# A weight's high and low parts for two blocks at once, where there is room for pairs of blocks

## The chip, the cores and the metric

The kernel runs on one core of one Trainium2 chip. The metric is the device time of one execution in microseconds, as the median of the runs.

## The reference

A backbone of two layers on 512 latent tokens and 256 context tokens, 1024 channels, all in float32. Layer 0 mixes the tokens with a bidirectional mLSTM, layer 1 with a bidirectional Mamba-2 SSD. Each layer ends with PEER, a channel mixer that picks for every token 16 of 16384 experts for each of 8 heads. Cut to the products in question:

```python
for i in range(DEPTH):                                   # 2
    ml, mc = modulation(c, ...), modulation(c_ctx, ...)  # silu(cond) @ ada_w[i] + ada_b[i], six rows each
    in_l, in_c = h_lat * (1 + ml[1]) + ml[0], h_ctx * (1 + mc[1]) + mc[0]
    # i = 0, mlstm: xm, z, o = h @ w_up; q, k = silu(conv(xm)) @ w_qk; v = xm @ w_v; ...; (...) @ w_down
    # i = 1, mamba2: z, xbc, dt = h @ w_in; ...; (...) @ w_out
    h_lat = layer_norm(ALPHA * h_lat + ml[2] * y_l, ...)
    h_lat = layer_norm(ALPHA * h_lat + ml[5] * peer_ffn(h_lat * (1 + ml[4]) + ml[3], ...), ...)
    # the context likewise, in layer 0 only

def block(xb):                                           # PEER, 128 tokens
    q = (xb @ wq).reshape(P_BLOCK, P_HEADS, 2, P_DK // 2)
    s = einsum('thcd,hcnd->thcn', q, sub_keys)           # 16 best keys of each half, then 16 best pairs
    act = gelu(einsum('td,thkd->thk', xb, u[idx]))
    return einsum('thk,thkd->td', gate * act, v[idx])
```

## The kernel before

**Products in three passes.** A float32 product is the sum of three passes of parts: an operand's high part is its value cast to fp32r, its low part is what is left. `mm3` (L211 to L213) issues high by high, high by low, low by high. So every weight is split on its way in. `wpair` (L169) does that for two blocks of 128 x 512 that one transfer brings: `raw2` (L152) allots one of three raw tiles [128, 2, 512] in the pool `wp` and starts the transfer on SP's queue (L155); then for each block by itself ACT casts the high part (`whi`, L176), and DVE or POOL subtracts it from the raw block (`wlo`, L178). A raw tile is free when its second subtraction is done.

**Room for parts.** `whi` and `wlo` are of one block each. There are three of each in `wp`, unless `more_parts` (L160) has opened a pool with more: `wpc` (9 blocks, L1441) for the context's first product, the modulation beside it and the context's w_v; `wpd` (9 blocks, L1428) for the latents' first product, which runs among the context's attention, so that the context's w_down and the context's wq use it too. The latents' last products take their first 16 blocks into the pool `dp` (`halves`, nb=16). The dense part of PEER takes v's blocks into three buffers of the pool `xp`.

**Which engine subtracts.** `los["eng"]` is a cycle of engines that each call of `next` moves on by one: "vvp" (two on DVE, one on POOL) in the context's first product and the modulation beside it (LO_U), DVE otherwise. uT's blocks of steps below 36 (UPX) go to POOL in both layers, and so do all of s_in's blocks of the context in layer 1 (SCP).

**Order.** Stages by the trace, in us: context's first product with modulation 45 to 268, its w_v to 372, its w_qk to 592; the context's attention with the latents' first product among it, then w_down and wq, to 1038; the latents' v, qk, attention and w_down to 2228, wq to 2424; PEER's prefix of layer 0 to 2905; its dense part to 3748; layer 1's context from 3735 to 3960, latents to 4515, wq to 4665; prefix to 5170, dense part to 6006. In a prefix (`peer_lat`, NPRE = 66 steps i2) the scores `u x` of 128 experts a step are made (`scores`, `mm3` with 128x384 outputs) while DVE picks the best pairs of every head (`select`, L829) and builds gate tables of one-hot products (L1012 to L1022, of which L1015 is POOL's); the fourth tile of tokens takes its experts' rows by gathers on POOL's queue (L860), weighted and added on DVE. In the dense part PE multiplies gated scores with v for all 128 steps, and makes the remaining 62 steps' scores. The planner that builds the program (`TileContext`) puts each engine's instructions in an order by its own estimate, with waits where a tile is reused. A pool opened with reuse_waits="tile" waits for single tiles of what lay on its bytes before; one without (those of `more_parts`) waits for every user of the pools that lay there.

## Time and profile before

| | us |
|---|---|
| median of three runs | 6019.12 |
| the three runs | 6018.73, 6019.12, 6024.26 |
| span of the profiled execution | 6006.3 |
| PE busy | 5316.2 (89%) |
| DVE busy | 4835.9 (81%) |
| ACT busy | 2269.3 (38%) |
| POOL busy | 2221.4 (37%) |
| cast to the high part (L176), 2032 instructions | 1227.3 |
| subtraction on DVE (L178), 1787 | 1245.3 |
| subtraction on POOL (L178), 245 | 340.6 |

The profile is of one execution on the chip; its span runs from the first to the last instruction. Busy times of different engines overlap, so they don't add up, and a share of the whole span is a mean over stages with different limits. What an instruction is worth is read in its stage: from what the other engines wait for there, and for how long.

### The profile page before, as it was taken

What the parts mean: (1) busy time and instruction counts of PE and PEld (TensorE: products, weight loads), DVE (VectorE), ACT (ScalarE), POOL (GpSimd) and SP (SyncE); (2) the same over time, 40 slices, a digit from 0 to 9 for tenths busy, and PEclk for the clock granted to TensorE, in tenths of its full rate; (3) what the DMA queues carried; (4) which work ended last, traced back from release to release, by engine and by line L of the source; (5) the groups of instructions that cost most, each with busy time, mean ns of one, the idle gap of its engine ahead of it and who ended that gap; (6) DMA issues with size and microseconds to landing.
All of it is one profiled execution on the core that took longest, in us unless ns stands there. A gap on an engine that the chain in (4) does not pass through costs nothing. (4 is left out here: it accounts for less than half of the span.)

```text
span 6006.3 us, 79377 instructions
## 1 busy us (share of the span) xinstructions
PE 5316.2 (89%) x25708; PEld 4369.6 (73%) x25708; DVE 4835.9 (81%) x11088; ACT 2269.3 (38%) x4219; POOL 2221.4 (37%) x1908
## 2 busy tenths in 40 slices
PE   6999999999997885888899999788878879799998
PEld 4788677766653464777778998676656779688997
DVE  6744668776677799999988988778877999798988
ACT  5543554232222332333333333443433334343333
POOL 1300001355534345564333445424341454433442
PEclk8999999999998897989999999799978989899999
DMA  6754455898879986456798999333334347898996
GB/s 215 248 183 163 155 181 158 296 332 299 310 249 322 339 304 224 138 168 201 256 343 315 349 335 328 100 95 104 99 103 127 105 142 228 275 345 318 342 342 234
DMA packets 655817, 1407.12 MB, mean 234 GB/s; under 512 B 62760, under 2 KB 237496, under 8 KB 650920
## 3 DMA queue, kind: packets, MB, share of 16 engines
q1 hardware_dynamic: 507944, 865.11, 42.9%
q0 software_dynamic: 147456, 536.94, 25.5%
q8 instruction: 202, 3.31, 0.2%
q14 instruction: 215, 1.76, 0.1%
HBM read 1278.10 MB, written 123.70 MB: 233 GB/s over the span
## 5 line engine op out<-in xcount | busy, mean ns | idle before, releaser
L176 ACT CAST whi<-raw 128x512 fp32r<-128x512 f32 x2032 | 1227.3, 619 | 1843.8 <-PE mm L212 614.4
L178 DVE TENSOR_TENSOR wlo<-raw,whi 128x512 fp32r<-128x512 f32 x1787 | 1245.3, 712 | 446.0 <-ACT whi L176 427.0
L860 POOL DMA_INDIRECT g<-in_u_dram,idx x512 | 638.8, 1248 | 1074.1 <-PE mx L213 276.8
L860 POOL DMA_INDIRECT g<-in_v_dram,idv x512 | 667.4, 1304 | 691.7 <-DVE acc L878 281.9
L878 DVE SCALAR_TENSOR_TENSOR acc<-g,act,acc 128x1024 f32<-128x1024 f32 x508 | 656.3, 1292 | 137.9 <-DMA g<-in_v_dram,idv 135.2
L867 DVE CUSTOM_DVE_ANT_0 g<-g,xb 128x1024 f32<-128x1024 f32 x512 | 626.3, 1227 | 149.4 <-DMA g<-in_u_dram,idx 148.4
L213 PE MATMUL sm<-pinh,wlo 128*128 128x384 f32 x2048 | 712.0, 349 | 30.3 <-POOL wlo L178 18.6
L211 PE MATMUL sm<-pinh,whi 128*128 128x384 f32 x2048 | 709.8, 347 | 5.8 <-ACT whi L176 3.6
L212 PE MATMUL sm<-pinl,whi 128*128 128x384 f32 x2048 | 705.5, 345 | 0.0
L178 POOL TENSOR_TENSOR wlo<-raw,whi 128x512 fp32r<-128x512 f32 x245 | 340.6, 1398 | 447.8 <-ACT whi L176 431.8
L829 DVE SCALAR_TENSOR_TENSOR oh<-iotc,bjf,g 128x50 f32<-128x50 f32 x1280 | 446.0, 397 | 0.2
L213 PEld LDWEIGHTS sm<-pinh,wlo 128*128 128x128 f32 x2048 | 395.6, 193 | 40.7 <-POOL wlo L178 22.5
L212 PE MATMUL mm<-wlo,wh 128*128 128x512 f32 x1024 | 399.6, 393 | 9.2 <-DVE wlo L178 9.2
L211 PEld LDWEIGHTS sm<-pinh,whi 128*128 128x128 f32 x2048 | 396.6, 194 | 12.8 <-ACT whi L176 4.7
L212 PEld LDWEIGHTS sm<-pinl,whi 128*128 128x128 f32 x2048 | 396.0, 193 | 5.5
L213 PE MATMUL mm<-whi,wl 128*128 128x512 f32 x1024 | 394.6, 392 | 3.1 <-DVE wl L189 3.0
L211 PE MATMUL mm<-whi,wh 128*128 128x512 f32 x1024 | 363.0, 396 | 33.6 <-ACT wh L188 29.5
L1015 POOL TENSOR_TENSOR oa<-oh,ct 128x512 bf16<-128x512 bf16 x192 | 249.5, 1310 | 293.7 <-DVE oh L1012 155.8
L212 PE MATMUL mm<-xcl,whi 128*128 128x256 f32 (+1 forms) x1024 | 349.0, 345 | 6.7 <-DVE xcl L189 6.7
L213 PE MATMUL mm<-xch,wlo 128*128 128x256 f32 (+1 forms) x1024 | 331.1, 348 | 21.7 <-DVE wlo L178 21.7
L211 PE MATMUL mm<-xch,whi 128*128 128x256 f32 (+1 forms) x1024 | 344.6, 349 | 5.0 <-ACT xch L188 4.0
L211 PE MATMUL mm<-inh,whi 128*128 128x512 f32 (+1 forms) x768 | 284.1, 374 | 9.7 <-ACT cva L404 4.9
(478 smaller groups left out, 11508.2 us busy)
## 6 DMA issues: line engine op xcount, KB each, us to landing
raw<-in_uT_dram SPq DMA_DIRECT2D x256, 512.0 KB
raw<-in_v_dram SPq DMA_DIRECT2D x256, 512.0 KB
raw<-in_w_qk_dram SPq DMA_DIRECT2D x128, 512.0 KB
raw<-in_ada_w_dram SPq DMA_DIRECT2D x96, 512.0 KB
raw<-in_w_up_dram SPq DMA_DIRECT2D x96, 512.0 KB
gD<-sg SPq DMA_DIRECT2D x48, 1024.0 KB
gtb<-gD SPq DMA_DIRECT2D x32, 1536.0 KB
raw<-in_s_in_dram SPq DMA_DIRECT2D x72, 512.0 KB
```

The lines of the kernel that those rows point to most:

```text
L176: nc.scalar.copy(hi, raw[:, u])
L178: (eng or next(los["eng"])).tensor_tensor(lo, raw[:, u], hi.bitcast(F32), OP.subtract)
L211: nc.tensor.matmul(o, sh, mh, start=start, stop=False)
L212: nc.tensor.matmul(o, sh, ml, start=False, stop=False)
L213: last["pe"] = nc.tensor.matmul(o, sl, mh, start=False, stop=stop)
L829: nc.vector.scalar_tensor_tensor(oh[:, k % 2], iotc, bjf[:, hd, k:k + 1], ci[:, hd], OP.is_equal, OP.mult, accum_out=fi[:, hd, k:k + 1])
L860: d = nc.gpsimd.indirect_dma_start(out=g_, out_offset=None, in_=tab, in_offset=bass.IndirectOffsetOnAxis(ap=ix[:, k:k + 1], axis=0))
L867: nc.vector.tensor_tensor_reduce(out=g_, in0=g_, in1=xb, scale=1.0, scalar=0.0, op0=OP.mult, op1=OP.add, accum_out=act[:, k:k + 1])
L878: nc.vector.scalar_tensor_tensor(acc, g_, act[:, k:k + 1], acc, OP.mult, OP.add)
L1015: (nc.gpsimd if GOP else nc.vector).tensor_tensor(oa, oh[:, 0], ct[:, 2, None, n].to_broadcast([P, P, 4]), OP.mult)
```

## The change

Where the parts go to a pool other than `wp`, `wpair` now makes them for both blocks of a transfer at once: one cast and one subtraction of 128 x 1024, into a `whi` and a `wlo` of [128, 2, 512], of which the two blocks are views. In `wp` they are made block by block as before. Pools count pairs now: `wpc` and `wpd` hold 4 pairs (WB = 4) for 9 blocks, `halves` 8 pairs for 16 blocks. New pools of pairs are opened: `wpq` (4) for the context's w_qk, `pw` (2) for PEER of the latents (wq and uT, in both layers), `scw` (2) for the context's s_in. `more_parts` restores the pool that was open before it. v's blocks go to `wp`. The cycle of engines moves on once for a pair. The diff, without comments that it takes out:

```diff
-WB = 9
+WB = 4
     def more_parts(es, name, bufs, side=None):
+        old = los.get("pool"), los.get("bufs")
         los.update(pool=es.enter_context(tc.tile_pool(name=name, bufs=1, side=side)), bufs=bufs)
-        es.callback(lambda: los.pop("pool"))
+        es.callback(lambda: los.update(pool=old[0], bufs=old[1]))
     def wpair(src, pool=None, eng=None, nb=None):
         raw = raw2(src)
-        pool = pool or los.get("pool", wp)
-        nb = nb or (los["bufs"] if pool is los.get("pool") else 3)
-        for u in range(2):
-            hi = pool.tile([P, 512], F32R, tag="whi", name="whi", bufs=nb)
-            nc.scalar.copy(hi, raw[:, u])
-            lo = pool.tile([P, 512], F32R, tag="wlo", name="wlo", bufs=nb)
-            (eng or next(los["eng"])).tensor_tensor(lo, raw[:, u], hi.bitcast(F32), OP.subtract)
-            yield hi, lo
+        pool = pool or los.get("pool") or wp
+        if pool is wp:
+            both = [(wp, 3, raw[:, u]) for u in range(2)]
+        else:
+            both = [(pool, nb or los["bufs"], raw)]
+        for pl, n, x in both:
+            hi, lo = [pl.tile(list(x.shape), F32R, tag=g, name=g, bufs=n) for g in ("whi", "wlo")]
+            nc.scalar.copy(hi, x)
+            (eng or next(los["eng"])).tensor_tensor(lo, x, hi.bitcast(F32), OP.subtract)
+            if pl is wp:
+                yield hi, lo
+            else:
+                for u in range(2):
+                    yield hi[:, u], lo[:, u]
@@ halves
-                        ws += wpair(wt[1, k:k + 2].rearrange("k p c -> p k c"), pool=dp, nb=16)
+                        ws += wpair(wt[1, k:k + 2].rearrange("k p c -> p k c"), pool=dp, nb=8)
@@ peer_lat
-        with tc.tile_pool(name="pt", bufs=1, reuse_waits="tile") as xp:
+        with tc.tile_pool(name="pt", bufs=1, reuse_waits="tile") as xp, ExitStack() as es_:
+            more_parts(es_, "pw", 2)
@@ dense
-            v = wpair(vs.rearrange("p (h c) -> p h c", h=2), pool=xp)
+            v = wpair(vs.rearrange("p (h c) -> p h c", h=2), pool=wp)
@@ ssd_ctx
-            with tc.tile_pool(name="scv", bufs=1, reuse_waits="tile") as q:
+            with tc.tile_pool(name="scv", bufs=1, reuse_waits="tile") as q, ExitStack() as es_:
+                more_parts(es_, "scw", 2)
@@ the context's w_qk
-    for _ in ml_qk(1, CTX):
-        pass
+    with ExitStack() as es_:
+        more_parts(es_, "wpq", WB)
+        for _ in ml_qk(1, CTX):
+            pass
```

## Rows read from the trace of the kernel before

**Rows 1.** The page: span; busy us (share), instructions of each engine.
```profile
span 6006.3 us, 79377 instructions
PE 5316.2 (89%) x25708; PEld 4369.6 (73%) x25708; DVE 4835.9 (81%) x11088; ACT 2269.3 (38%) x4219; POOL 2221.4 (37%) x1908
```

**Rows 2.** By stage: window, length; PE, PEld, DVE, ACT, POOL us; PEclk, DMA, GB/s.
```profile
45.00:268.00 223.00, 184.26 (x1092) 147.09 (x1093) 164.64 (x272) 127.34 (x255) 78.66 (x52) 0.91 0.69 223
...
2424.00:2905.00 481.00, 401.67 (x2374) 378.75 (x2373) 463.51 (x1622) 180.83 (x320) 258.40 (x255) 0.91 0.57 176
...
3500.00:3600.00 100.00, 100.00 (x504) 91.15 (x503) 89.69 (x109) 38.99 (x72) 47.36 (x36) 1.00 0.92 327
...
4665.00:5170.00 505.00, 428.11 (x2517) 401.81 (x2515) 489.70 (x1895) 186.07 (x333) 260.61 (x259) 0.91 0.55 171
...
3735.00:3960.00 225.00, 177.67 (x959) 147.97 (x958) 166.70 (x292) 100.74 (x205) 108.75 (x101) 0.85 0.35 117
```

**Rows 3.** Durations by line: count, ns min/median/max, first and last start, forms.
```profile
L176 ACT CAST whi<-raw x2032: 601/620/657, 8.5 to 5976.9; 128x512 fp32r<-128x512 f32 x185
...
L188 ACT CAST yh<-yfc x32: 394/406/410, 808.0 to 895.9; 128x256 fp32r<-128x256 f32 x32
...
L178 DVE TENSOR_TENSOR wlo<-raw,whi x1787: 631/685/1880, 9.1 to 5977.5; 128x512 fp32r<-128x512 f32 x199
...
L178 POOL TENSOR_TENSOR wlo<-raw,whi x245: 1252/1294/5399, 52.1 to 4947.4; 128x512 fp32r<-128x512 f32 x123
...
L1310 DVE TENSOR_TENSOR bcs<-bcs,dt_acs x32: 1206/1226/2054, 4004.5 to 4477.6; 128x1024 f32<-128x1024 f32 x32
...
L1140 POOL TENSOR_TENSOR S<-S,dt_eal x64: 605/796/2182, 3891.3 to 4453.3; 128x256 f32<-128x256 f32 x64
```

**Rows 4.** In order of time, 120 to 127: start, us, engine, line, what.
```profile
120.05 0.28 PE L211 MATMUL mm<-inh,whi 128*128 128x256 f32 x1
120.08 0.37 SPq L155 DMA_DIRECT2D raw<-in_w_up_dram  x1
...
120.17 0.28 PE L212 MATMUL mm<-inl,whi 128*128 128x256 f32 x1
...
124.15 1.14 ACT L176 CAST whi<-raw 128x512 fp32r<-128x512 f32 x2 [1.02 <-DMA raw<-in_w_up_dram]
...
124.81 1.29 DVE L178 TENSOR_TENSOR wlo<-raw,whi 128x512 fp32r<-128x512 f32 x2 [1.48 <-ACT whi L176]
...
126.13 0.37 SPq L155 DMA_DIRECT2D raw<-in_ada_w_dram  x1
```

**Rows 5.** The same, 2555 to 2559, of DVE and of POOL.
```profile
2555.81 1.33 DVE L829 SCALAR_TENSOR_TENSOR oh<-iotc,bjf,g 128x50 f32<-128x50 f32 x1
...
2558.32 0.26 DVE L829 SCALAR_TENSOR_TENSOR oh<-iotc,bjf,g 128x50 f32<-128x50 f32 x1
...
2555.78 2.54 POOL L178 TENSOR_TENSOR wlo<-raw,whi 128x512 fp32r<-128x512 f32 x2
```

**Rows 6.** Groups by line, 2424 to 2905: count, busy us, mean ns, idle before.
```profile
L829 DVE SCALAR_TENSOR_TENSOR oh<-iotc,bjf,g 128x50 f32<-128x50 f32 x411 | 161.8, 442 | 0.1
...
L178 DVE TENSOR_TENSOR wlo<-raw,whi 128x512 fp32r<-128x512 f32 x62 | 52.1, 842 | 1.5 <-ACT whi L176 1.5
...
L1015 POOL TENSOR_TENSOR oa<-oh,ct 128x512 bf16<-128x512 bf16 x90 | 116.6, 1307 | 147.7 <-PE mx L1022 55.4 <-DVE oh L1012 47.2 <-DVE oh L829 14.1
```

**Rows 7.** Who waited for whom, 45 to 268: us in total, times, longest.
```profile
ACT whi L176 <- DMA raw<-in_w_up_dram: 33.5, 29, 2.9
...
ACT whi L176 <- DMA raw<-in_ada_w_dram: 20.3, 15, 2.4
...
ACT whi L176 <- PE mm L212: 9.3, 10, 2.0
```

**Rows 8.** Groups by line, 3735 to 3960.
```profile
L178 POOL TENSOR_TENSOR wlo<-raw,whi 128x512 fp32r<-128x512 f32 x48 | 68.9, 1448 | 84.4 <-ACT whi L176 83.3 <-DVE st L408 0.3
```

## The prediction

> **What bounds the kernel now.** I read the page's first part, then the busy time by stage, then the groups by line, and at last single instructions. The page [rows 1] has PE busy 89% of the 6006.3 us and DVE 81%, which says little, since the stages differ [rows 2]. Two kinds of stage matter. In the dense stretches (3500 to 3600 stands for both layers) PE is busy the whole 100 us: preparation of weights is hidden there and can only lose. In the two prefixes (2424 to 2905 and 4665 to 5170) PE is busy 402 of 481 and 428 of 505 us, but DVE 464 of 481 and 490 of 505: there DVE is late last, and a microsecond off DVE is a microsecond off the stage. The reader should see two more: the context's first product (45 to 268) where no engine is full (PE 184 of 223, DVE 165), and the context's part of layer 1 (3735 to 3960) with PE 178 of 225, where every low part is made on POOL.
>
> Preparing weights costs 2032 casts and 1787 + 245 subtractions [rows 3]. By the code 1016 transfers of two blocks feed them. The change pairs 576 transfers (w_up of both streams 96, modulation 32, the context's w_v 32, w_qk 64, w_down 16, all wq 48, uT 256, the context's s_in 24, half of s_out 8) and leaves 440 in single blocks, among them all 256 of v. Of the 576 low parts POOL makes 123 (every third of the first 80, 72 of the prefixes, 24 of s_in), DVE 453.
>
> **The prices.** One cast: 620 ns at 512 elements and 406 at 256 [rows 3], so by that slope 0.62 + 2 x 0.214 = 1.05 us at 1024 (estimate). Two single casts in a row take 1.14 [rows 4], so a pair saves 0.09. A subtraction on DVE: two singles in a row take 1.29 us [rows 4]; one instruction of 1024 elements, two inputs and four-byte types takes 1.226, the median of L1310 [rows 3]. A pair saves 0.06. Taken alone the single lasts 0.685 [rows 3], and then it would be 0.144: the other end. I take 0.06, because in a stage where DVE is 97% busy its instructions stand in a row and overlap. On POOL: 1294 ns at 512, 796 at 256 [rows 3], so 1.294 + 2 x 0.498 = 2.29 at 1024 (estimate); two singles in a row take 2.54 [rows 5], and a pair saves 0.25. Over the kernel that is 53 us of ACT, 29 of DVE and 31 of POOL less busy time, nearly all of it where it isn't last.
>
> [...]
>
> **The prefixes.** 60 pairs go to DVE there (30 steps in each layer): 60 x 0.064 = 4 us less; ends 0 and 60 x 0.144 = 9. The POOL steps act on DVE too. A 128x50 step of L829 takes 0.26 us, but 1.33 when it begins with the first of two POOL subtractions in a row, and it ends as that one ends [rows 5]: POOL's instruction of 1.27 us keeps DVE's two-input instruction out for 1.07. In the first prefix L829 averages 442 ns over 411 instructions, so it loses 411 x 0.182 = 75 us, and L178 on DVE another 62 x 0.157 = 10 us; with 90 of L1015 [rows 6] and 72 subtractions (36 steps by two) that is 85 / 162 = 0.52 us for one POOL instruction. Two singles in a row keep DVE out for 2.14 us, one pair 2.29 - (1.27 - 1.07) = 2.09. So where DVE is pressing all the time 72 pairs give back 72 x 0.05 = 4 us. Ends: all of POOL's saved time comes to DVE, 72 x 0.25 = 18 us gained; or a single loses only its 0.52, that is 0.55 less than the full block, and the pair loses 2.09 - 0.55 = 1.54 against 1.04, 72 x 0.50 = 36 us lost. I take the 4, nearest to the row of two in a row.
>
> [...]
>
> Sum of the prefixes: 4 + 4 = 8 us less. PE there waits for DVE and POOL more than for itself, so what is late next is again DVE.
>
> **The context's first product.** Three raw buffers hold the transfers. One issued at 120.08 is cast at 124.15, its two subtractions run from 124.81 to 126.10, and the next transfer into that buffer goes at 126.13 [rows 4]: 1.95 us of holding, and no slack. ACT waits there for w_up's transfers 29 times and for modulation's 15 times, 54 us in all, for PE's release only 10 times [rows 7]. So the ring of three is late last in 44 of 80 transfers. With a pair the subtraction starts only when the whole cast is done: 1.05 + 0.04 + 1.23 = 2.32 on DVE, and 1.05 + 0.04 + 2.29 = 3.38 on POOL. Before, a transfer with a POOL block held 1.95 (first block) or 1.14 + 0.04 + 1.29 = 2.47 (second), and one on DVE alone 1.95: on average 2.12. After, (2 x 2.32 + 3.38) / 3 = 2.67. That is 0.55 more for each round of three, 0.18 for each transfer: 44 x 0.18 = 8 us lost. Ends: 0, if the buffered 4 pairs (8 blocks where there were 9) cover it, and 80 x 0.18 = 15. Queued behind a POOL pair's low part here are PE's modulation products, and behind those in PE's order the next products of w_up.
>
> **The context's part of layer 1.** POOL gets 24 pairs for 48 singles of 1448 ns [rows 8], 24 x (2.90 - 2.29) = 15 us less, and convolution steps on DVE are kept out less. Against it: there were three single buffers, now two pairs. PE needs 24 products of 0.12 us [rows 4], 2.9 us for a pair, and a buffer's round is 1.05 + 0.04 + 2.29 + 2.9 = 6.3, over two buffers 3.14: 0.26 more than PE wants, 24 x 0.26 = 6 us. I take 0, ends -8 (half of the 15) and +6.
>
> **The rest.** The context's v and qk stages, the latents' up and the peer's wq: PE or long chains are last, and 4 pairs or 2 pairs for 9 or 3 blocks change the depth little; 0, ends -6 and +6. Dense: 0, because PE is full; if that cover failed, 124 steps of a pair that comes 0.36 later would cost up to 45 us, but raw and weights there stand ready several us ahead, PE being full. The new pools (wpq, pw, scw) lie on bytes that earlier pools have left, and their first cast has to wait for those pools' last users; the trace doesn't show such a wait. Bounds: 0, or one cast and one subtraction uncovered at each of four openings, 4 x 2.3 = 9; I take 2. v's parts move from the peer's pool into wp, with three buffers again: 0. SP's queue has the same transfers in the same order; POOL's queue holds its gathers and L1015 behind a longer instruction, which is in the lock's ends above. The planner orders all queues anew; I have no row for that and leave 10 us either way.
>
> Sum: -8 + 8 + 0 + 0 + 2 = +2 us on the profiled execution. Its span is 6006.3 us and its own time lies within the three runs shown, 6018.73 to 6024.26, some 13 us above the span; the sum is set on their median, 6019.12, so 6021.
>
> **The rivals.** *Fixed costs count in full* (chance 0.28): every instruction saved on DVE in the prefixes is worth 0.144 us and POOL's shorter total comes to DVE, 9 + 18 = 27 us, with the first product unharmed: 5992. For it: DVE's 97%. Against it: the rows of instructions in a row, which overlap. [...] *The pair's low part comes late* (chance 0.30, slower): the first product of a pair waits for the whole cast and the whole subtraction. Its place is the context's first product, where the ring of three is the bound; from 2.12 us of holding on each further 0.1 us costs 0.03 us a transfer, and if all 80 are bound so, 15 us; s_in's two buffers add 6; with no gain in the prefixes 6040. For it: 54 us of waits for transfers. Against it: in the other 36 transfers something else is late. *The change doesn't do what it says where it would count* is part of the forecast: v's 256 transfers, a quarter, stay single, and the paired uT of the dense stretches lies under a full PE.
>
> **How the numbers follow.** Within 0.2% (12 us, about what a measurement of this kernel can tell from no change) has 0.42 and is the forecast, 6021; faster 0.28, slower 0.30. The range reaches to both rivals and the planner's 10 us beyond part of them, 5994 to 6046; what is left out, the lock's 36 us and an uncovered dense stretch, I put at under 2 in 10. The forecast's own range is 6007 to 6031.
>
> **What would show it.** Right: casts of 128x1024 near 1.05 us, subtractions near 1.23 on DVE and 2.29 on POOL; DVE's busy time in the prefixes down by some 2 to 6 us each, with L829 at an unchanged mean; the stretch from 45 to the first w_v product some 8 us longer, with more waiting of ACT for transfers; dense stretches as long as before. Wrong: prefixes shorter by over 10 us each (then a pair blocks DVE less than its length says), or longer with L829 above 480 ns (then the longer lock costs), a first product that is no longer, or dense stretches in which PE waits for low parts.

## The result: slower by 1.0%

The changed kernel takes 6069.76 us (median of four runs, 6062.91 to 6072.6) against 6018.92 of the kernel before beside it: a ratio of 1.0099, 95% interval 1.0082 to 1.0116. (The ratio is the measurement's own; the quotient of the two medians is 1.0084, and one of the four runs of before took 5989.46 us where the other three took 6018.73 to 6024.26.) The forecast was 6021, with 5994 to 6046 as its range: the time lies outside, on the slower side. The page of after, its first lines:

```profile
span 6061.1 us, 77541 instructions
PE 5328.7 (88%) x25708; PEld 4361.0 (72%) x25708; DVE 4817.8 (79%) x10635; ACT 2186.3 (36%) x3643; POOL 2200.9 (36%) x1785
```

Beside [rows 1], ACT has lost 83 us of work, DVE 18, POOL 21 (forecast 53, 29 and 31), and the span is 55 us longer. Line numbers of after are 3 to 9 higher: the cast L176 is L180, the subtraction L178 is L181, the products L211 to L213 are L218 to L220, `select`'s L829 is L836, L1015 is L1023, L1022 is L1030 and the transposes of inputs L316 are L323; in the experiments they are higher by a few more. The instructions cost what was forecast, but for POOL's. Durations by line, as in [rows 3]:

```profile
L180 ACT CAST whi<-raw x1456: 602/622/1080, 8.7 to 6031.6; 128x512 fp32r<-128x512 f32 x109, 128x1024 fp32r<-128x1024 f32 x73
...
L181 DVE TENSOR_TENSOR wlo<-raw,whi x1334: 642/693/3355, 9.4 to 6032.3; 128x512 fp32r<-128x512 f32 x125, 128x1024 fp32r<-128x1024 f32 x66
...
L181 POOL TENSOR_TENSOR wlo<-raw,whi x122: 2330/2396/4427, 52.7 to 4991.7; 128x1024 fp32r<-128x1024 f32 x122
```

A pair on POOL takes 2.396 us (forecast 2.29), so it saves 0.14 us against two singles in a row ([rows 5], 2.54) and not 0.25. The 576 casts of pairs alone have a mean of 1.047 (forecast 1.05).

**Where the time went.** I cut both traces at the first product of each stage on PE, so that a stage lasts from its own first product to that of the next. The table has these lengths for the stages that matter, in us. "b2" is a second trace of the kernel before, from the experiments: what it differs by from the first is what a difference must exceed.

| stage | before | b2 | after |
|---|---|---|---|
| context's first product, modulation | 201.5 | 201.9 | 221.7 |
| context's w_v | 100.8 | 100.8 | 105.0 |
| context's w_qk, up to the second tile of the latents' input | 237.5 | 237.9 | 243.5 |
| context's attention, and its w_down | 258.9 | 258.8 | 262.2 |
| latents' w_qk | 590.4 | 584.9 | 590.5 |
| prefix, layer 0 | 500.8 | 498.9 | 507.3 |
| prefix, layer 1 | 489.1 | 489.5 | 492.2 |
| dense with v alone, both layers | 555.9 | 549.1 | 572.1 |
| dense with scores, both layers | 1066.4 | 1064.8 | 1058.9 |
| context of layer 1 | 233.6 | 231.8 | 236.8 |

So the largest loss of one stage is the context's first product, the prefixes are longer where they should be shorter, and a dozen microseconds are lost where pools open. Two traces of one program differ by 5 to 7 us in the latents' w_qk and in the dense stretch with v alone, so of those little can be said from one trace; the first product, w_v, w_qk and the prefixes repeat within 2 in these two. (Six kernels that are like after up to there scatter by 6 in the first product, as shown below, so one length of it is good to some 6.) The windows of after, columns as in [rows 2]:

```profile
70.00:292.00 222.00, 190.30 (x1104) 150.12 (x1103) 143.86 (x211) 117.21 (x174) 62.64 (x25) 0.96 0.64 207
...
2469.00:2976.00 507.00, 406.47 (x2418) 383.23 (x2416) 491.81 (x1773) 173.36 (x266) 255.34 (x221) 0.88 0.58 179
3560.00:3660.00 100.00, 100.00 (x504) 90.20 (x503) 86.45 (x93) 36.40 (x59) 45.83 (x35) 1.00 0.94 337
4732.00:5225.00 493.00, 403.20 (x2397) 377.17 (x2396) 472.97 (x1734) 166.90 (x259) 245.80 (x222) 0.91 0.58 177
```

and the same stretches of before, cut in the same way:

```profile
75.00:276.00 201.00, 183.38 (x1100) 148.50 (x1100) 150.97 (x261) 123.28 (x249) 75.42 (x50) 0.97 0.70 227
...
2440.00:2941.00 501.00, 402.39 (x2411) 379.99 (x2410) 482.70 (x1739) 185.83 (x330) 259.83 (x256) 0.89 0.59 180
4690.00:5179.00 489.00, 403.11 (x2395) 380.99 (x2393) 468.10 (x1763) 179.75 (x323) 258.04 (x257) 0.90 0.57 178
```

In the first product every engine that prepares weights has less to do than before, and the stretch is 21 us longer, with 207 GB/s for 227: nothing is full, something waits. In the dense stretch PE is busy all 100 us as in [rows 2]. In the prefixes DVE, the engine that should gain, is busy for 9 and 5 us more (in layer 0 with work of the stage ahead, see PEER).

### The profile page after: what moved, and what is told of

Read it like the earlier page. It is cut to its first block, busy times and chain, and to the rows that moved or that the text cites. A ratio compares the mean times of both kernels' runs of the same rounds, so it can differ in the third digit from the quotient of the medians.

```text
span 6061.1 us, 77541 instructions
## 1 busy us (share of the span) xinstructions
PE 5328.7 (88%) x25708; PEld 4361.0 (72%) x25708; DVE 4817.8 (79%) x10635; ACT 2186.3 (36%) x3643; POOL 2200.9 (36%) x1785
## 5 line engine op out<-in xcount | busy, mean ns | idle before, releaser
L180 ACT CAST whi<-raw 128x512 fp32r<-128x512 f32 (+1 forms) x1456 | 1137.5, 789 | 1584.9 <-PE mm L219 560.1
L181 DVE TENSOR_TENSOR wlo<-raw,whi 128x512 fp32r<-128x512 f32 (+1 forms) x1334 | 1176.2, 891 | 426.2 <-ACT whi L180 405.7
L885 DVE SCALAR_TENSOR_TENSOR acc<-g,act,acc 128x1024 f32<-128x1024 f32 x508 | 674.0, 1327 | 147.2 <-DMA g<-in_v_dram,idv 143.3
L220 PE MATMUL sm<-pinh,wlo 128*128 128x384 f32 x2048 | 707.4, 346 | 14.6 <-POOL wlo L181 10.1
L218 PE MATMUL sm<-pinh,whi 128*128 128x384 f32 x2048 | 705.2, 344 | 16.4 <-ACT w L985 15.0
L181 POOL TENSOR_TENSOR wlo<-raw,whi 128x1024 fp32r<-128x1024 f32 x122 | 303.3, 2488 | 460.2 <-ACT whi L180 424.7
L836 DVE SCALAR_TENSOR_TENSOR oh<-iotc,bjf,g 128x50 f32<-128x50 f32 x1280 | 444.6, 398 | 0.1
L218 PEld LDWEIGHTS sm<-pinh,whi 128*128 128x128 f32 x2048 | 397.9, 194 | 25.3 <-ACT w L985 17.3
L220 PEld LDWEIGHTS sm<-pinh,wlo 128*128 128x128 f32 x2048 | 398.0, 194 | 23.4 <-POOL wlo L181 13.4
L220 PE MATMUL mm<-whi,wl 128*128 128x512 f32 x1024 | 399.4, 396 | 0.0
L218 PE MATMUL mm<-whi,wh 128*128 128x512 f32 x1024 | 364.5, 398 | 26.1 <-ACT wh L195 20.4
L220 PE MATMUL mm<-xch,wlo 128*128 128x256 f32 (+1 forms) x1024 | 346.4, 348 | 24.2 <-DVE wlo L181 24.0
L1023 POOL TENSOR_TENSOR oa<-oh,ct 128x512 bf16<-128x512 bf16 x192 | 243.9, 1281 | 330.6 <-DVE oh L1020 214.4
L218 PE MATMUL mm<-xch,whi 128*128 128x256 f32 (+1 forms) x1024 | 349.3, 349 | 4.8 <-ACT xch L195 4.8
L1030 PE MATMUL mx<-og,oa 128*128 128x128 f16 x1536 | 206.9, 296 | 109.4 <-DVE og L1025 86.7
```

The costliest lines, as they stand in the source:

```text
L180: nc.scalar.copy(hi, x)
L181: (eng or next(los["eng"])).tensor_tensor(lo, x, hi.bitcast(F32), OP.subtract)
L218: nc.tensor.matmul(o, sh, mh, start=start, stop=False)
L220: last["pe"] = nc.tensor.matmul(o, sl, mh, start=False, stop=stop)
L836: nc.vector.scalar_tensor_tensor(oh[:, k % 2], iotc, bjf[:, hd, k:k + 1], ci[:, hd], OP.is_equal, OP.mult, accum_out=fi[:, hd, k:k + 1])
L885: nc.vector.scalar_tensor_tensor(acc, g_, act[:, k:k + 1], acc, OP.mult, OP.add)
```

## The experiments

Each kernel is timed beside the kernel before on its own chip, whose median went from 5999 to 6019 us between chips; so ratios are compared, not times. Where a variant keeps single blocks in a pool, `more_parts` gets a last argument `False` and `wpair` runs its old loop for that pool. I begin with the measure of a trace.

**b2.** The kernel before, unchanged.

> The kernel before, unchanged, for a second trace of it. What the stages of two traces of one program differ by is the size below which a difference between stages says nothing. If the trace shown was an ordinary one, every stage agrees within 3 us, and the stages that are longer in the changed kernel and its variants by 4 to 7 us (w_v, the context's w_down, both prefixes) stay so against this trace too. If it was a lucky one, those differences go.

1.0001 (0.9985 to 1.0017). The table above has its stages: w_v, w_down and the prefixes stand, two stages scatter by 5 to 7 us, more than the 3 expected.

### The context's first product

**u_c.** The changed kernel with nine single blocks in `wpc`.

```diff
-    more_parts(wpc, "wpc", WB, "right")
+    more_parts(wpc, "wpc", 9, "right", False)
```

> The changed kernel, with the context's first product, the modulation beside it and the context's w_v again in nine single blocks; all else as changed. Theory A (three raw buffers are the bound of that stretch, and a pair holds one longer): the stretch from the first to the last product with the context's input falls from 208 back to near 186 us, and the time by 20 to 24, to about 6048. Theory B (the loss of 50 us is spread over all stages, by the planner's new order): the time stays within 8 us of 6070.

1.0076 (1.0059 to 1.0092): a quarter of the loss. The stretch is 203.3 us by the cut of the table (the expectation's 208 and 186 are of another cut): the loss of this place is the pairs' and is gone with them. But three quarters of the whole stay, so it is spread over other places too, as theory B has it: neither alone holds. w_v stays at 104.6 although its blocks are single again, so that its 4 us are not the pairs' of w_v.

**ring4.** A fourth raw buffer in a pool of its own while `wpc` is open.

```diff
+        rp_ = next(ring) if "xpool" in ring_ else wp     # every fourth transfer: the pool "rw", one buffer
-        raw = wp.tile([P, 2, 512], F32, tag="raw", name="raw", bufs=3)
+        raw = rp_.tile([P, 2, 512], F32, tag="raw", name="raw", bufs=3 if rp_ is wp else 1)
```

> The changed kernel with a fourth raw buffer while the context's first product, modulation and w_v run, pairs kept. Theory A (the ring of raw buffers): with four in turn the waits of ACT for transfers fall, the stretch loses 15 to 25 us, about 6050. Rival (PE waits for the whole cast and the whole subtraction of a pair, however early the transfer is there): no gain in the stretch, 6065 to 6075, and PE's waits for low parts as before.

1.0075 (1.0058 to 1.0091), the stretch 199.8 us: with pairs as they are, one more raw buffer gives back all that they cost. The rival (PE waits for late parts whatever the transfers do: no gain) falls as the account of the whole; with four buffers pairs still take 9 us more than single blocks (b_r4, below). Waits of ACT for transfers from 45 us to near the end of this stretch (284 and 271), of after

```profile
ACT whi L180 <- DMA raw<-in_w_up_dram: 36.3, 27, 3.8
...
ACT whi L180 <- DMA raw<-in_ada_w_dram: 30.2, 26, 5.0
```

and of ring4 (us in total, times, longest):

```profile
ACT whi L185 <- DMA raw<-in_w_up_dram: 17.0, 14, 5.6
...
ACT whi L185 <- DMA raw<-in_ada_w_dram: 14.4, 12, 5.0
```

66.5 us of waiting in after ([rows 7]: 53.8 before) and 31.4 with four buffers.

**c_v.** The changed kernel with no low part on POOL there.

```diff
-LO_U = "vvp"
+LO_U = "v"
```

> The changed kernel with no low part on POOL in the context's first product and the modulation beside it (the cycle vvp made v). Theory A: a POOL pair holds its raw buffer 3.6 us, always the same one of three, a DVE pair 2.3 when POOL is quiet; with DVE alone the mean hold falls from 3.3 to 2.4 and a round of the three buffers from 8.5 to about 7.4, so the stretch loses 20 us: 6050. Rival (DVE becomes the bound when it makes all 80 low parts, 27 of them more, 33 us on top of some 165 busy in 222): no gain, 6065 to 6075.

1.0073 (1.0048 to 1.0098), the stretch 197.3 us. DVE has room for all low parts (busy 129.6 of the 180 us from 70 to 250), so the rival falls. Groups by line and form, DVE's pairs in the stretch (70 to 284 and 70 to 268), of after

```profile
L181 DVE TENSOR_TENSOR wlo<-raw,whi 128x1024 fp32r<-128x1024 f32 x50 | 70.3, 1413 | 59.2 <-ACT whi L180 54.1 <-PE mm L226 5.0
```

and of c_v:

```profile
L182 DVE TENSOR_TENSOR wlo<-raw,whi 128x1024 fp32r<-128x1024 f32 x78 | 95.1, 1220 | 50.0 <-ACT whi L181 46.4 <-PE mm L221 3.1
```

1.220 us without POOL (forecast 1.23), 1.413 with it: a pair on POOL holds DVE's pairs up as well as its own buffer. One round of after shows it, in order of time on each queue and engine:

```profile
176.99 0.38 SPq L155 DMA_DIRECT2D raw<-in_w_up_dram  x1
...
178.19 0.38 SPq L155 DMA_DIRECT2D raw<-in_ada_w_dram  x1
...
179.70 0.37 SPq L155 DMA_DIRECT2D raw<-in_w_up_dram  x1
...
181.51 1.05 ACT L180 CAST whi<-raw 128x1024 fp32r<-128x1024 f32 x1 [3.10 <-DMA raw<-in_w_up_dram]
182.86 1.05 ACT L180 CAST whi<-raw 128x1024 fp32r<-128x1024 f32 x1 [0.30 <-DMA raw<-in_ada_w_dram]
184.36 1.05 ACT L180 CAST whi<-raw 128x1024 fp32r<-128x1024 f32 x1 [0.46 <-DMA raw<-in_w_up_dram]
...
182.69 2.36 POOL L181 TENSOR_TENSOR wlo<-raw,whi 128x1024 fp32r<-128x1024 f32 x1 [5.72 <-ACT whi L180]
...
183.94 3.33 DVE L181 TENSOR_TENSOR wlo<-raw,whi 128x1024 fp32r<-128x1024 f32 x2 [4.27 <-ACT whi L180]
...
185.08 0.37 SPq L155 DMA_DIRECT2D raw<-in_ada_w_dram  x1
...
186.16 0.37 SPq L155 DMA_DIRECT2D raw<-in_w_up_dram  x1
187.30 0.37 SPq L155 DMA_DIRECT2D raw<-in_ada_w_dram  x1
```

Three transfers go out within 2.7 us, then none for 5.4, until POOL's pair ends at 185.05 and frees its buffer; DVE's two pairs take 3.33 us where two at 1.22 would take 2.44.

**res9.** Every third pair on POOL as before, but not always in the same buffer.

```diff
-LO_U = "vvp"
+LO_U = "vvpvpvpvv"
```

> The changed kernel with the same share of POOL in the context's first product, every third pair, but in the order vvpvpvpvv, so that POOL's pair falls into each of the three raw buffers in turn and not always into the same. Theory A1 (the ring goes at the pace of its slowest buffer, since SP's queue issues in order and every POOL pair comes to the same buffer): a round falls from 8.5 to near 7.7 us and the stretch loses 12 to 18 of its 20 us. Theory A2 (the mean hold of a pair sets the round, as in my sum): the mean hold is the same, the stretch within 4 us of 222.

1.0082 (1.0063 to 1.0101), the stretch 213.6 us. Six kernels whose program is that of after up to here (after, u_w, w_split, w_half, w_s4, u_s) have 215.4 to 221.7, mean 218.4: some 5 us won, which is neither theory's number. That POOL always meets the same buffer is a small part at most.

**b_v, b_r4, b_v_r4.** The kernel before, single blocks everywhere, without POOL there (the edit of c_v), with the fourth raw buffer there (the edit of ring4), and with both.

> The kernel before, single blocks everywhere, with no low part on POOL in the context's first product and the modulation beside it. If the ring of three raw buffers sets that stretch (a transfer with a POOL block holds its buffer 2.5 to 3.2 us, one on DVE alone 1.95 when it need not wait), the mean hold falls from 3.0 to 2.4, a round from 7.8 to 7.1, and the stretch loses 14 to 20 us against before: a ratio of 0.997. If DVE becomes the bound with 53 more subtractions (36 us), nothing is won or up to 10 us lost: 1.000 to 1.002.

> The kernel before with the fourth raw buffer in the context's first product, modulation and w_v, and POOL left in (vvp). If the ring is late there whoever subtracts, the stretch falls from 202 to some 186 us, as it did by taking POOL out, and the ratio to before is 0.997; if POOL's blocking of DVE is what counts and not the ring, it stays above 196, and 1.000.

> The kernel before with single blocks everywhere, no POOL in the context's first product and modulation, and a fourth raw buffer there. If the ring is still what is late there with DVE alone, the stretch falls from 186 (before 202) by another 5 to 10 us; if PE, which needs 173 us, and ACT's and DVE's chains are now late, by under 4. In the whole time a gain of 0.1 to 0.4% against before, if the planner's new order gives nothing back; the kernel without the fourth buffer showed 0.9995 although its stretch was 16 us shorter.

b_v: the stretch 185.8 us, 16 shorter than before as expected, yet 0.9995 (0.9982 to 1.0008) in the whole: other stages gave it back, and which did is not to be told from stages that scatter by 5 to 7. b_r4: 190.8 us, between its two expectations, and 0.9972 (0.9962 to 0.9982). b_v_r4: 181.7 us, 4 below b_v and so near the end of "under 4", and **0.9971** (0.9960 to 0.9982), with b_r4 the fastest of all, 0.3% below the kernel before and without a single pair.

The ring in numbers. For some 70 transfers of each kernel, from 66 us to 240 to 264 (before its stretch ends): how long a transfer holds its buffer (from its first cast to the end of its last subtraction), the time from its issue to its first cast, and the time from its issue to that of the third after it, all means in us.

| kernel | hold | issue to cast | three transfers | stretch |
|---|---|---|---|---|
| before | 3.04 | 4.59 | 7.76 | 201.5 |
| after | 3.28 | 5.05 | 8.51 | 221.7 |
| u_c, single blocks | 3.10 | 4.57 | 7.83 | 203.3 |
| c_v, pairs, no POOL | 2.49 | 4.89 | 7.41 | 197.3 |
| b_v, single, no POOL | 2.46 | 4.59 | 7.09 | 185.8 |
| b_v_r4, and four buffers | 2.79 | 5.89 | 6.57 | 181.7 |

80 transfers pass: (8.51 - 7.76) / 3 x 80 = 20 us, as measured; for b_v (7.09 - 7.76) / 3 x 80 = -18, measured -16. For c_v it gives -9, measured -4, and for b_v_r4 -32, measured -20: there the ring is no longer all that is late. u_w, whose program is that of after here, has 3.28, 4.72 and 8.17, so the time from issue to cast scatters too. Pairs and single blocks without POOL hold a buffer alike, and still c_v is 11.5 us longer than b_v: its casts come 0.3 us later after the issue. ACT's waits for PE to leave a buffer don't explain it, 11.8 us in c_v over this stretch against 9.3 in before [rows 7]; it stays open.

### Where pools open

**q_right.** `wpq` on the other side of the memory.

```diff
-        more_parts(es_, "wpq", WB)
+        more_parts(es_, "wpq", WB, "right")
```

> The changed kernel with the pairs' pool of the context's w_qk (wpq) on the other side of the memory, so that it doesn't lie on the bytes where the latents' input is loaded. Theory C (on the left side it keeps the latents' first loads until w_qk is over): the transposes of the latents' input no longer wait 22 us in all at the start of that stage but 10 to 14, and the time falls by 6 to 10 us, about 6062. If the pool's place doesn't matter: within 4 us of 6070.

The w_qk stage falls from 243.5 to 237.4, as expected, and with it the transposes' wait shown below; the time does not show it, 1.0114 (1.0097 to 1.0131) against 1.0099. The mechanism in order of time, in after:

```profile
623.71 0.64 SPq L1418 DMA_DIRECT2D res<-in_x_dram  x1
...
631.16 1.23 DVE L318 TENSOR_TENSOR big<-res,row 128x1024 f32<-128x1024 f32 x1 [0.41 <-DMA res<-in_x_dram]
...
633.70 1.97 PE L323 MATMUL sm<-ident,big 128*128 128x128 f32 x8 [11.69 <-DVE big L319]
```

and in before the same loads:

```profile
7.12 0.44 SPq L1409 DMA_DIRECT2D res<-in_x_dram  x1
66.85 0.33 SPq L1409 DMA_DIRECT2D res<-in_x_dram  x1
```

Before, the latents' first tiles were loaded 600 us ahead. With `wpq` on the left their place is taken until w_qk is over, and PE stands 11.69 us. All kernels with the first load near 7 us (before, b2, q_right, u_d, d5, b_v, b_r4, b_v_r4, best) have 233.7 to 238.0 us for w_qk, the ten with it after 600 us 241.3 to 248.5: 7 us, by the place of a pool. But the early loads have a price at the start, among the transfers that the first product waits for. With three raw buffers it begins at 73.4 to 77.1 us in the six kernels that load early (75.8 in q_right) and at 67.5 to 70.3 in the nine that load late (70.3 in after). So some 6 of the 7 us come back there, which fits that the time of q_right shows nothing.

The 4 us of w_v come from the same pool, but not from its place (q_right keeps them, 104.3). In order of time at its end, of after

```profile
388.54 2.94 ACT L180 CAST whi<-raw 128x1024 fp32r<-128x1024 f32 x3
...
391.38 1.07 ACT L529 COPY vT<-sm 128x512 f32<-128x512 f32 x2
392.51 3.59 PE L466 MATMUL sm<-vT,wgv 128*16 128x256 f32 x8 [1.80 <-ACT vT L529]
```

and of before:

```profile
373.50 0.59 ACT L522 COPY vT<-sm 128x512 f32<-128x512 f32 x1 [0.71 <-PE sm L1130]
...
374.46 0.59 ACT L522 COPY vT<-sm 128x512 f32<-128x512 f32 x1 [0.37 <-PE sm L1130]
374.94 1.02 ACT L188 CAST xch<-st 128x256 fp32r<-128x256 f32 x3
375.10 1.90 PE L459 MATMUL sm<-vT,wgv 128*16 128x256 f32 x8 [0.26 <-ACT vT L522]
```

Before, w_qk's first blocks went to `wp` and were made while w_v ran. Now the casts of three pairs stand in ACT's queue ahead of the copies that the gates need, and PE waits for those, 1.80 us for 0.26. The rest is a wait of 0.82 us for w_qk's first product, and PE's 453 products of w_v keep it busy for 102.4 us where they took 100.5, at a mean granted clock of 0.97 for 1.00. Kernels with `wpq` have 104.2 to 105.8 us for w_v, those without 100.8 to 103.3.

**u_d and d5.** The latents' first product, the context's w_down and its wq in nine single blocks, and in five pairs.

```diff
-                more_parts(es_, "wpd", WB)
+                more_parts(es_, "wpd", 9, None, False)         # u_d
+                more_parts(es_, "wpd", 5)                      # d5
```

> The changed kernel with the latents' first product, the context's w_down and its wq again in nine single blocks. If four pairs are too few where three streams of weights share them, the stretch of the context's w_down (110 us before, 116 or 117 with pairs) comes back to 110 or 111 and the ratio to before falls by 0.001, to 1.009. If that stretch is longer for another reason: 116, and 1.010.

> The changed kernel with five pairs in place of four for the latents' first product, the context's w_down and its wq. If the stretch of the context's w_down is 116 to 117 us and not 110 because four pairs are too few for two streams of weights, it falls to 111 to 113. If a pair's parts come too late there whatever the depth, 116.

u_d: 1.0074 (1.0046 to 1.0102); d5: 1.0089 (1.0072 to 1.0105). The w_down stretch comes back in both, 110.8 and 110.6 us for 116.8. But it was not the loss that I took it for. Windows of this stretch, of before, after and d5:

```profile
810.00:920.00 110.00, 103.03 (x449) 82.48 (x447) 75.16 (x146) 60.79 (x119) 2.15 (x1) 0.98 0.60 192
```

```profile
832.00:949.00 117.00, 111.18 (x473) 89.45 (x473) 74.82 (x125) 60.64 (x95) 1.94 (x1) 0.97 0.60 188
```

```profile
832.00:942.00 110.00, 103.91 (x453) 83.43 (x451) 70.96 (x118) 55.65 (x89) 1.35 (x1) 0.99 0.60 189
```

PE has 473 instructions in it in after, 449 and 453 in the others: work of the latents' product that ran in the stage ahead (the context's attention, 3 us shorter in after) came over. With that stage the difference is 3 us. Both kernels' larger pool also lets the latents' loads go at 7 us again, and their w_qk takes 233.7 and 236.7.

**mend.** Pairs in layer 0's first stages alone, no POOL and four raw buffers in the first product, `wpq` on the right, five pairs for the latents: the edits of c_v, ring4, q_right and d5 in one, without `pw` and `scw`, with sixteen single blocks in `halves` and v in `xp`.

> Pairs only in layer 0's first stages (context's first product, modulation, w_v, w_qk, latents' first product, context's w_down and wq), with each cause of loss found there taken away: no POOL and a fourth raw buffer in the first product, wpq on the other side, five pairs for the latents; PEER, s_in and s_out in single blocks as before. If ring, place and depth are the causes, the context's first product, w_v and w_qk together fall to 520 to 526 us (before 540, changed 570), the latents' loads are issued near 7 us again, and the ratio is 0.996 to 0.999. If the pair as such costs there, it stays over 1.000. Single blocks with the fourth buffer and no POOL had 523 us and 0.9971: pairs save nothing beyond that unless this goes below.

0.9975 (0.9963 to 0.9986). First product, w_v and w_qk together take 533.8 us: 6 less than before (539.8), 36 less than after (570.1), but 11 more than the single blocks of b_v_r4 with the same ring (523.1). The latents' loads went at 584 us only, so the place was not mended. With ring and POOL alike, pairs still cost 7 us in the first product (189.0 against 181.7); in the whole time mend and b_v_r4 are not told apart.

### PEER

**u_w, w_split, w_half, w_s4.** The changed kernel without the pool `pw` (v in `xp`, as before); with POOL's part of a pair in two subtractions; with every engine's part in two; and with four single blocks on the bytes of the two pairs.

```diff
-            more_parts(es_, "pw", 2)
+            more_parts(es_, "pw", 4, None, False)          # w_s4
     (in wpair, for the pool pw; in w_split where the engine is POOL, in w_half always)
-            e.tensor_tensor(lo, x, hi.bitcast(F32), OP.subtract)
+            for u in range(2):
+                e.tensor_tensor(lo[:, u], x[:, u], hi[:, u].bitcast(F32), OP.subtract)
```

> The changed kernel without the pool of pairs in PEER (pw): wq and uT in single blocks in wp, v in three buffers of xp, as before; all else as changed. If the pairs are what makes the prefixes longer (501 to 507 us and 489 to 493), both fall back, by 6 and 4 us, the two stretches with scores lose the 4 us each that they won, and the time stays within 6 us of the changed kernel's ratio to before, 1.010. If POOL's longer lock costs (the upper end of my range, 36 us), the ratio falls to 1.005 or less. If the prefixes are longer by the planner's order alone, they stay at 507 and 493.

> The changed kernel in which POOL's part of a pair in PEER (72 pairs of uT) is worked out as two subtractions of 512 elements; cast and DVE's pairs as changed. Theory P1 (the prefixes are longer since POOL's 2.4 us instruction holds back what is queued behind it, the gate tables' products L1023 on POOL above all): the prefixes come back from 507 and 493 to some 501 and 489. Theory P2 (the pair's parts come later and two pairs hold no more than four blocks, so PE and the tables collide whatever POOL's grain is): they stay at 505 to 508 and 492 to 495. The time itself moves too little to tell, 0 to 10 us.

> The changed kernel with every low part in PEER's pool of pairs worked out in two halves, on DVE as on POOL; only the cast is of 1024. If PE's waiting for a whole subtraction makes the prefixes longer, they come back to 501 and 489; if two pairs are too shallow, so that the cast of a pair waits until PE has done with all of the pair two before, they stay at 505 to 508 and 492 to 495.

> The changed kernel with its pool for PEER (pw) on the same bytes and v in wp, as changed, but with four single blocks in it where two pairs were, each cast and subtracted by itself. Theory W1 (the pair as such: its parts come late and whole, in a pool of two): the prefixes come back, 507 to some 501 and 493 to some 489, and the stretches with scores lose their 3 us. Theory W2 (the pool's place, or v in wp): the prefixes stay at 505 to 508 and 492 to 495. Ratio to before 1.006 under W1 as in the kernel without the pool, 1.010 under W2.

| | ratio | prefix, layer 0 | layer 1 |
|---|---|---|---|
| 8 kernels without `pw` in the prefix | | 500.0 (498.5 to 502.7) | 489.5 (489.1 to 490.2) |
| 11 kernels with pairs in `pw` | | 507.5 (502.8 to 512.5) | 493.6 (492.1 to 495.6) |
| u_w | 1.0061 (1.0036 to 1.0085) | 499.5 | 489.4 |
| w_split | 1.0102 (1.0084 to 1.0120) | 509.1 | 494.1 |
| w_half | 1.0085 (1.0065 to 1.0106) | 508.6 | 495.6 |
| w_s4 | 1.0107 (1.0085 to 1.0128) | 506.2 | 489.9 |

(u_w, w_split and w_half are among the kernels of the means.) By these cuts the pool costs 7.5 + 4.1 = 12 us. POOL's grain is not it, nor the late subtraction: neither split brings the prefixes back. In layer 1 it goes with the pairs (w_s4 489.9), in layer 0 it stays without them (506.2): there it is the pool, its place or what the planner makes of it. So neither theory of w_s4 holds for both. u_w's ratio fell by 0.004, some 23 us and far more than the 6 of its expectation; it also moves v.

Most of the 12 us is work that changed its stage, as with w_down. wq, the stage ahead of the prefix, is shorter with the pool: 123.4 us for 128.0 in layer 0, 103.1 for 105.2 in layer 1 (means of the same kernels), and steps of `select` that ran there in before run in the first prefix of after (L829 below, 503 for 492). From wq's first product to the dense part the means are 630.9 us (626.8 to 636.1) for 628.0 (626.3 to 630.5), and 596.7 (594.4 to 599.2) for 594.7 (593.5 to 595.9): 5 us in both layers, and the groups overlap. Groups by line and form of the first prefix, of before

```profile
L829 DVE SCALAR_TENSOR_TENSOR oh<-iotc,bjf,g 128x50 f32<-128x50 f32 x492 | 182.3, 420 | 0.1
...
L1022 PE MATMUL mx<-og,oa 128*128 128x128 f16 x768 | 101.3, 296 | 48.8 <-DVE og L1017 35.1 <-DVE bj L793 6.6 <-POOL oa L1015 5.8
...
L178 POOL TENSOR_TENSOR wlo<-raw,whi 128x512 fp32r<-128x512 f32 x70 | 94.6, 1359 | 40.9 <-ACT whi L176 39.7 <-DVE oh L829 0.9
...
L178 DVE TENSOR_TENSOR wlo<-raw,whi 128x512 fp32r<-128x512 f32 x63 | 53.6, 853 | 0.8 <-ACT whi L176 0.8
```

and of after:

```profile
L836 DVE SCALAR_TENSOR_TENSOR oh<-iotc,bjf,g 128x50 f32<-128x50 f32 x503 | 185.8, 423 | 0.0
...
L1030 PE MATMUL mx<-og,oa 128*128 128x128 f16 x768 | 103.3, 296 | 59.6 <-DVE og L1025 43.4 <-POOL oa L1023 11.4 <-DVE ih L996 2.9
...
L181 POOL TENSOR_TENSOR wlo<-raw,whi 128x1024 fp32r<-128x1024 f32 x35 | 86.7, 2478 | 24.6 <-ACT whi L180 21.8 <-DVE oh L836 2.4 <-issue 0.2
...
L180 ACT CAST whi<-raw 128x1024 fp32r<-128x1024 f32 x65 | 68.0, 1046 | 108.2 <-PE sm L219 59.7 <-issue 25.0 <-POOL wlo L181 16.7
...
L181 DVE TENSOR_TENSOR wlo<-raw,whi 128x1024 fp32r<-128x1024 f32 x30 | 37.4, 1248 | 1.9 <-ACT whi L180 1.9
```

L829's mean is 420 ns before and 423 after: by that the lock on DVE (for how long a POOL instruction keeps it out, 1.07 us for one of 1.27 in [rows 5]) has neither grown nor shrunk, though POOL's subtractions take 8 us less, 86.7 for 94.6. What has grown in layer 0 is PE's wait for the gate tables (L1022 for DVE's and POOL's halves), 48.8 to 59.6 us; in w_s4 it is 61.2:

```profile
L1031 PE MATMUL mx<-og,oa 128*128 128x128 f16 x768 | 100.2, 296 | 61.2 <-DVE og L1026 51.9 <-POOL oa L1024 8.5 <-ACT sg L1033 0.7
```

In layer 1 that wait has not grown, and what has is the wait of the scores' products for ACT to read their sums (w, L977 and L985). The second prefix (4690 to 5179 and 4732 to 5225), of before

```profile
L829 DVE SCALAR_TENSOR_TENSOR oh<-iotc,bjf,g 128x50 f32<-128x50 f32 x512 | 208.3, 448 | 0.0
...
L1022 PE MATMUL mx<-og,oa 128*128 128x128 f16 x768 | 101.0, 296 | 50.5 <-DVE og L1017 45.6 <-DVE ic L986 2.7 <-ACT sg L1024 1.5
...
L211 PE MATMUL sm<-pinh,whi 128*128 128x384 f32 x528 | 188.1, 356 | 1.5 <-ACT whi L176 1.1 <-ACT w L977 0.4
```

and of after:

```profile
L836 DVE SCALAR_TENSOR_TENSOR oh<-iotc,bjf,g 128x50 f32<-128x50 f32 x512 | 205.0, 441 | 0.0
...
L1030 PE MATMUL mx<-og,oa 128*128 128x128 f16 x768 | 103.7, 296 | 49.8 <-DVE og L1025 43.4 <-ACT sg L1032 2.6 <-POOL oa L1023 1.9
...
L218 PE MATMUL sm<-pinh,whi 128*128 128x384 f32 x528 | 186.2, 353 | 10.5 <-ACT w L985 10.5
```

**best.** b_v_r4 with pairs in the dense part alone (v in `wp`).

```diff
-            with tc.tile_pool(name="pd", bufs=1, reuse_waits="tile") as dp:
+            with tc.tile_pool(name="pd", bufs=1, reuse_waits="tile") as dp, ExitStack() as es_:
+                more_parts(es_, "pw", 2)
```

> The kernel before with no POOL in the context's first product and modulation, a fourth raw buffer there, and pairs in the dense part of PEER alone (uT's 62 last steps, v in wp as in the change; prefixes, wq and all else in single blocks). The two stretches with scores were 3.5 us shorter with pairs: -7 against the kernel with the fourth buffer. If the 3 to 16 us that the stretch of v alone in layer 1 was longer by come from v's place in wp, they show here too and eat that; if they come from the prefix's pairs, they don't. Ratio to before 0.995 to 1.000.

0.9993 (0.9983 to 1.0003): slower than b_v_r4. The stretches with scores are shorter by 7 us, as expected (1056.1 against 1063.4), those with v alone longer by 11 (565.0 against 554.1). Six kernels with v in `xp` and single blocks in the prefix and dense part have 549.1 to 559.6 there, a seventh, mend, 562.8; thirteen with v in `wp` 556.1 to 575.7, mean 565.9. The two groups overlap, and v's place was not changed alone, so that it costs some 10 us is likely, not shown. Another 4 us go with it, in groups that don't overlap: from the last product of layer 1's s_out to the first of wq it takes 24.5 to 24.8 us in the seven kernels with v in `xp` and 28.7 to 30.9 in the thirteen with v in `wp`, w_s4 and best among them, whose wq is in single blocks. Why is open.

**u_s.** Single blocks for the context's s_in and for `halves`.

```diff
-                more_parts(es_, "scw", 2)
-  pool=dp, nb=8)
+  pool=dp, nb=16)
```

> The changed kernel with single blocks for s_in of the context (no pool scw) and sixteen single blocks in halves; all else as changed. If the pairs make the context's part of layer 1 and the end of s_out's product longer, the first falls from some 237 us (mean of the kernels with them) to 232 to 234, the second from 132 to some 129.5; if these are only the planner's order, they stay. The time itself: 1.009 against 1.010, too little to tell.

1.0094 (1.0071 to 1.0116). The context of layer 1 falls to 231.8 us, but mend, which has single blocks there too, has 237.5: from this stage alone nothing follows. Together with the latents' part behind it, from the first product of s_in of the context to the first of s_out, the groups part: the eight kernels without `scw` have 626.7 to 633.1 us, mean 630.0 (u_s 628.2, mend 632.2); the twelve with it 634.9 to 641.7, mean 638.1. u_w, without `pw`, is among the long ones (640.0) and u_s, with it, among the short, so the pool of pairs for s_in costs some 8 us; u_s's own ratio, with its interval, can't show that. Whether it is the pair, two buffers for three or the pool's place was not tried. From the last product of s_out to the first score product, wq included, it takes 131.2 us in u_s and 131.7 in after: sixteen single blocks bring nothing there.

## Why the prediction was wrong

**The prices were right but for POOL's, the places were not.** Cast 1.047 us for 1.05, DVE 1.220 for 1.23 (c_v, no POOL beside it), POOL 2.396 for 2.29. Of the 576 pairs POOL makes 122 and not 123, since every third of 80 is 26. The instructions got cheaper, and little that sets the end got shorter.

**The first product: right mechanism, 8 us for 17.** (17 is the mean of the six kernels, 218.4, less 201.7 of before and b2.) The rival that the pair's low part comes late named this place, and its condition held: of the 18 transfers issued from 126 to 172 us of after 16 go within 0.03 us of the end of the subtraction that frees their buffer, and a round of three that is 0.75 us longer gives, over all 80, the 20 us measured; so nearly all are bound, not 44 of 80. I had counted only the transfers for which ACT waited last. Its price per transfer was off the other way: I had a hold of 2.12 us going to 2.67, from durations of blocks that nothing held up; measured are 3.04 and 3.28. The rest of the 0.75 us that a round is longer is between issue and cast (4.59 to 5.05 us), which my sum did not have; in the round shown, whose three transfers go out together, it is 4.5 to 4.7, so what makes it longer is not shown. For the rival's time I gave 6040; it falls short for the losses elsewhere.

**The prefixes: -8 forecast, nothing won.** With wq they are 5 us longer, by their own first products 12. The 4 us of DVE's own did come, and more: the low parts on DVE take 39.4 us in the first prefix of after where they took 53.6, and 45.3 for 52.0 in the second (L178 and L181 of DVE in the windows above; in after the 30 pairs and three single blocks). The other 4 us, of the lock, rested on 2.29 us for POOL's pair; with 2.396 the same sum keeps DVE out for 2.20 us where two singles kept it out for 2.14, and loses 4. Measured is no change that counts: L829 420 and 423 ns in layer 0, 448 and 441 in layer 1. The lock shows in the first product too, where DVE's pairs take 1.413 us beside POOL (after) and 1.220 without (c_v).

The step that failed is that DVE's share alone sets the stage ("a microsecond off DVE is a microsecond off the stage"): 14 and 7 us less of subtractions made neither stage shorter. PE waits there for a chain through DVE, POOL, PE and ACT: in layer 0 its wait for the tables grew by 11 us; in layer 1 its waits for low parts fell by 9 (L213 15.5 us, L220 6.3), and those for ACT grew by 10. Whether that chain got later because weights came in lumps or because the order of work changed stays open.

**The openings: +2 forecast, some 11 measured, of which 6 come back.** I had looked at the first cast of a new pool. Right in kind for w_v (4 us, in part in ACT's queue), but the larger part (7 us) is that a pool keeps the next stage's early loads from its bytes: the latents' first load goes at 623.71 us of after, for 7.12 before. I took "the new pools lie on bytes that earlier pools have left" for the whole of it, and did not look for what else lay there: the loads of the latents' input at 7 and 67 us were in the trace of before. That they come late makes the first product begin some 6 us earlier, so the openings in layer 0 cost some 5.

**The rest at nothing.** The dense stretches with scores gained a little, 4 us in both layers together (mean 1062.0 of the twelve kernels with pairs there, 1065.7 of the seven without); I had 0. v's move from the peer's pool into `wp` I put at 0, since it has three buffers again; it may cost 10, and 4 more before wq of layer 1. The context's part of layer 1 I put at 0, with 6 us lost as the end; with the latents' part behind it, which I did not look at, it loses 8. Four pairs in the context's w_down cost 3.

The losses that the traces separate (17 + 11 + 5 + 4 + 8 + 3) and the likely 10 of v make 58, less the 6 at the start and 4 of the scores 48; the medians differ by 51, the ratio says 60. My base was low in one point: I read 13 us between the span of before and its own time, from runs that didn't include the profiled one; in b2 and after the two are 1.8 us apart, so the profiled execution of before was one of some 6008 us. The sum was set on the median, so the forecast was not moved by it.

## What to carry to other kernels

Here fewer, longer instructions took 83 us of work from ACT, 18 from DVE and 21 from POOL, and the kernel became 1.0% slower: what got shorter was seldom what the stage waited for last, so look for that first. Where the longer step stood in front of a ring of three buffers, a round of the ring went from 7.76 to 8.51 us; look at how long a buffer is held and how many there are. In the kernel before, one more raw buffer made that stretch of 200 us 11 us shorter (b_r4, 0.3% in the whole time), and with it and no POOL, halving the number of casts there won nothing (189.0 us in mend, 181.7 in b_v_r4). Before a pool is opened, look for what the program loads early on the bytes that it or its neighbours will take: here w_qk lost 7 us by it. And before a stage is called longer, add the stage ahead of it: the prefixes were 12 us longer by their own first products, 5 with wq.

## What the runs showed that I had not expected

- Two traces of one program differ by 5.5 us in one stage (latents' w_qk, 590.4 and 584.9) and 7 in another (dense with v alone in layer 0, 280.2 and 272.9), while most agree within 2.
- A subtraction on POOL of 1024 elements takes 2.396 us, less than two of 512 in a row ([rows 5], 2.54), and DVE's L829 beside it takes about as long as before (423 ns for 420 in layer 0, 441 for 448 in layer 1).
- Taking POOL out of a stretch made it 16 us shorter (b_v) and the whole kernel no faster, 0.9995 (0.9982 to 1.0008).
